# Gate and up products of four feed-forward parts as seven products of quarters instead of eight

## The chip, the cores and the metric

The kernel runs on one core of a Trainium2 chip. The core has five engines that run side by side, each with its own queue of instructions: TensorE (PE in the profile; its weight loads are PEld), VectorE (DVE), ScalarE (ACT), GpSimd (POOL) and SyncE (SP), which here only issues DMA transfers. Instructions of one engine start in order; between engines they wait for semaphores. Data lie in SBUF (128 partitions) or, as results of TensorE, in PSUM (8 banks). The metric is the time of one execution on the device in microseconds; the comparison uses the median of several executions.

## What is computed

A stack of two transformer-like layers over 512 tokens plus 16 meta tokens in front (528), then a second kind of block over the 512 tokens, all in float32 with a model width of 1024. What matters here are its five feed-forward parts, each with a hidden width of 2816:

```python
def swiglu(x, w_gu, w_down):
    gate, up = jnp.split(x @ w_gu, 2, axis=-1)
    return (jax.nn.silu(gate) * up) @ w_down

h = h + 0.5 * swiglu(rms_norm(h, ffn1_norm[l]), ffn1_w_gu[l], ffn1_w_down[l])   # before each mixer
h = h + 0.5 * swiglu(rms_norm(h, ffn2_norm[l]), ffn2_w_gu[l], ffn2_w_down[l])   # behind each mixer
...
x = x + (jax.nn.silu(h2 @ w_ffn_gate[l]) * (h2 @ w_ffn_up[l])) @ w_ffn_down[l]  # in the second block
```

## The kernel before

Activations lie feature-major: a tile holds 128 features on the partitions and all tokens as columns. The feed-forward parts are called a0 and b0 (layer 0), a1 and b1 (layer 1) and c (second block). a0, b0 and a1 run over 528 tokens, in two pieces of 264 columns; b1 and c over 512 in one piece. Their order in time is a0, b0, a1, b1, c, with a mixer ahead of b0, one ahead of b1 and the second block's attention and state-space branches ahead of c.

*Precision.* TensorE is fed in a format that holds fewer bits than float32. So every operand is split in a high part (`whi`, `xh`, `gh`: a copy into the short format) and a remainder (`wlo`, `xl`, `gl`: original minus high part), and each product of a k tile of 128 takes three matmuls (`mm3`, lines 356 to 358): high x high, high weight x low input, low weight x high input.

*The feed-forward part* (`ffn`). A hidden tile j (0 to 21, 128 hidden features) takes the gate product and the up product, 8 k tiles each, in banks of their own. The input is not normed yet; VectorE multiplies both results by the norm's factor R per token as it takes them out of PSUM (`scaled`, line 444), ScalarE makes Silu, VectorE multiplies (line 455), ScalarE and VectorE split the result into gh and gl. After tiles 0 to 8, 9 to 15 and 16 to 21 stand the down products of 8, 7 and 7 hidden tiles, which add to the residual h. R comes from a sum over the squares, which a matmul with ones does after the products of tile 0 (line 396).

*The weights* (`run`). They come in chunks of 128 x 1024 (8 k tiles by 128 columns, 512 KB) into three raw buffers in turn. ScalarE makes the high half (line 218), GpSimd or, for each third chunk, VectorE the remainder (line 319), into four pairs of buffers in turn. `ahead` issues these splits up to four chunks ahead of use, and behind each split the load that takes the raw buffer just read. SP issues loads in order; each waits until its buffer's last reader is done.

What sets the order: the program is a list of items (a hidden tile, a group of down products), each with its chunks; the framework then places the instructions of each engine in an order of its own, worked out beforehand, so code that is written later can stand earlier in an engine's queue.

## Time and profile before

| | us |
|---|---|
| median of 3 runs | 3302.76 |
| lowest, highest | 3295.20, 3303.64 |
| span of the profiled execution | 3300.4 |
| TensorE busy in it | 3250.9 (99%) |
| VectorE, ScalarE, GpSimd busy | 1645.8, 1166.3, 1145.8 |

The profile records one execution; the page has no other time for it than the span from its first to its last instruction. A row of a group gives the line of the kernel, the engine, the operation, out<-in with names, the shape, the count, then busy time in us and the mean of one in ns, and the idle time of the engine just before, with what ended it. Matmuls overlap each other, so their own durations are longer than the time from one start to the next. In the timeline the first number is the start in us, the second the duration.

### The profile page before, as it was taken

The page shows a single profiled execution, that of the slowest core. Times are in us where ns is not written, and L with a number is a line of the kernel's source. Part 1 is how long each engine was busy: PE and PEld are TensorE (multiplying, and loading weights), DVE is VectorE, ACT ScalarE, POOL GpSimd, SP SyncE. Part 2 cuts the span into 40 slices and gives each one's busy share as a digit, 9 for nine tenths or more (in the row PEclk, how much of TensorE's full clock was granted, in tenths as well). Part 3 has the DMA queues.
Part 4 walks back from the last instruction along what each step waited for, and adds up shares of the span by engine and source line. Part 5 has one row for each costly group of instructions (what it writes and reads, how often), then busy time and mean ns, then how long its engine had stood idle before and what let it go on. Part 6 is the DMA issues. An engine that isn't in the chain of part 4 may idle for free. (4 is left out here: it accounts for less than half of the span.)

```text
span 3300.4 us, 49937 instructions
## 1 busy us (share of the span) xinstructions
PE 3250.9 (99%) x20794; PEld 2878.9 (87%) x20794; DVE 1645.8 (50%) x2687; ACT 1166.3 (35%) x1777; POOL 1145.8 (35%) x614
## 2 busy tenths in 40 slices
PE   9999999999999999999999999999999889999999
...
PEclk9999999999999999999998999999999989999999
...
GB/s 183 122 107 110 93 88 39 46 52 65 90 90 96 84 95 87 95 90 90 85 88 58 46 48 63 96 95 96 91 94 148 109 87 58 71 91 95 93 95 80
DMA packets 106514, 289.43 MB, mean 88 GB/s; under 512 B 23088, under 2 KB 32304, under 8 KB 106288
## 3 DMA queue, kind: packets, MB, share of 16 engines
...
## 5 line engine op out<-in xcount | busy, mean ns | idle before, releaser
L319 POOL TENSOR_TENSOR wlo<-raw,whi 128x1024 fp32r<-128x1024 f32 (+1 forms) x346 | 840.6, 2430 | 1797.1 <-ACT whi L218 1758.0
L218 ACT ACTIVATE whi<-raw 128x1024 fp32r<-128x1024 f32 (+1 forms) x504 | 522.6, 1040 | 1536.3 <-PE bank L357 807.0
L356 PE MATMUL bank<-xh,whi 128*128 128x264 f32 (+1 forms) x2816 | 881.1, 313 | 3.7 <-DVE t L444 3.1
L357 PE MATMUL bank<-xl,whi 128*128 128x264 f32 (+1 forms) x2816 | 880.8, 313 | 2.7 <-DVE xl L377 2.6
L358 PE MATMUL bank<-xh,wlo 128*128 128x264 f32 (+1 forms) x2816 | 881.4, 313 | 1.3 <-POOL wlo L319 1.3
L356 PEld LDWEIGHTS bank<-xh,whi 128*128 128x128 f32 x2816 | 530.9, 189 | 37.7 <-DVE t L444 3.5
L357 PEld LDWEIGHTS bank<-xl,whi 128*128 128x128 f32 x2816 | 531.2, 189 | 36.4 <-DVE xl L377 3.5
L358 PEld LDWEIGHTS bank<-xh,wlo 128*128 128x128 f32 x2816 | 530.6, 189 | 33.2 <-POOL wlo L319 1.5
L444 DVE TENSOR_TENSOR t<-bank,R 128x264 f32<-128x264 f32 (+1 forms) x352 | 163.5, 494 | 576.2 <-PE bank L358 571.5
L358 PE MATMUL bank<-gh,wlo 128*128 128x264 f32 (+1 forms) x1408 | 439.6, 312 | 0.0
L356 PE MATMUL bank<-gh,whi 128*128 128x264 f32 (+1 forms) x1408 | 439.3, 312 | 0.0
L357 PE MATMUL bank<-gl,whi 128*128 128x264 f32 (+1 forms) x1408 | 439.1, 312 | 0.0
L541 PE MATMUL bank<-xh,whi 128*128 128x264 f32 (+2 forms) x1224 | 428.0, 350 | 0.0
L541 PE MATMUL bank<-xl,whi 128*128 128x264 f32 (+2 forms) x1224 | 423.6, 346 | 3.0 <-DVE xl L377 3.0
L541 PE MATMUL bank<-xh,wlo 128*128 128x264 f32 (+2 forms) x1224 | 419.5, 343 | 0.0
L356 PEld LDWEIGHTS bank<-gh,whi 128*128 128x128 f32 x1408 | 264.8, 188 | 16.3 <-issue 0.4
L357 PEld LDWEIGHTS bank<-gl,whi 128*128 128x128 f32 x1408 | 264.8, 188 | 16.1
L358 PEld LDWEIGHTS bank<-gh,wlo 128*128 128x128 f32 x1408 | 264.8, 188 | 15.7
L541 PEld LDWEIGHTS bank<-xl,whi 128*128 128x128 f32 (+1 forms) x1224 | 233.9, 191 | 28.9 <-issue 6.5
L541 PEld LDWEIGHTS bank<-xh,whi 128*128 128x128 f32 (+1 forms) x1224 | 233.8, 191 | 25.1 <-issue 5.8
L541 PEld LDWEIGHTS bank<-xh,wlo 128*128 128x128 f32 (+1 forms) x1224 | 233.5, 191 | 24.9 <-issue 8.1
L501 DVE SCALAR_TENSOR_TENSOR h<-bank,h 128x264 f32<-128x264 f32 (+1 forms) x192 | 89.7, 496 | 331.8 <-PE bank L358 331.1
...
## 6 DMA issues: line engine op xcount, KB each, us to landing
raw<-in_w_dram SPq DMA_DIRECT2D x423, 512.0 KB, 3.5
...
```

The costliest lines, as they stand in the source:

```text
L218: i = self.e.activation(out, in_, func, **kw)
L319: e.tensor_tensor(lo[:, :n], t[:, :n], hi[:, :n].bitcast(F32), op=OP.subtract)
L356: mm(p, hi[:, wk, :m], xh[k][:, c0:c1], start=start, stop=False)
L357: mm(p, hi[:, wk, :m], xl[k][:, c0:c1], start=False, stop=False)
L358: mm(p, lo[:, wk, :m], xh[k][:, c0:c1], start=False, stop=stop)
L444: nc.vector.tensor_tensor(t[:, a:b], p, st["R"][:, a:b], op=OP.mult)
L501: nc.vector.scalar_tensor_tensor(hv, q, alpha, hv, op0=OP.mult, op1=OP.add)
L541: self.nc.tensor.matmul(at["ps"], w[:, k0 + k, :m], xx[k][:, a:b], start=k == t == 0, stop=k == nk - 1 and t == 2)
```

## The change

In a1, b0, b1 and c, hidden tiles 5 to 21 are computed in another way. Gate and up weights of a hidden tile together are one matrix of 1024 x 256, the input one of 1024 x tokens. Each is seen as 2 x 2 quarters: the weights by k tiles 0 to 3 and 4 to 7 and by gate and up, the input by k tiles and by first and second half of the tokens. Of the 2 x 2 quarters of the result (gate and up, for the two halves of the tokens) eight quarter products would be the plain way; here seven are taken, of sums and differences of quarters, and the results are put together from partial sums.

- In the input: `sums`, once per part, in tiles 1 to 4 while these run the plain way. Per pair of k tiles (k, k + 4) it makes the normed input itself (x0, x1, gain and R applied), four combinations (ta, tb), and splits all into high and low parts.
- In the weights: `split_seven`, per hidden tile, in four parts: part 0 is chunk g as it is (VectorE), part 1 the half-chunk sums s1 and s2, part 2 s3 and s4 (sums on VectorE, high halves on ScalarE, remainders on VectorE), part 3 half of chunk u (remainder on GpSimd). One buffer pair holds two quarters. A raw buffer is given back only with parts 2 and 3.
- The products: `unit`, in four items per hidden tile. Bank b1 takes four of the seven products one on top of the other; after the first three ScalarE copies what stands there (tu twice, zu), before TensorE may add the next. b3 takes two, b2 one. VectorE puts c1 (gate) and c2 (minus up) together; R is no longer applied here.

The diff, without the lines that only take comments away:

```diff
     def run(self):
         order = [c for it in self.prog for c in it.chunks]
+        loads = [c for u in order for c in (([u] if isinstance(u, str) else u[1:3]) if isinstance(u, str) or u[0] == 0 else [])]
         self.split_of = {}
         raws = {}
+        S = {}
         n_dma = n_split = used = 0
+        nc = self.nc
         def dma(i):
-            idx, nk, m, _ = CHUNKS[order[i]]
+            idx, nk, m, _ = CHUNKS[loads[i]]
             t = self.wp.tile([128, 1024], F32, tag=f"raw{i % self.RAW}", name=f"raw_{i}")
             self.nc.sync.dma_start(t[:, :nk * m], self.ins["w"][idx, :, :nk * m])
-            raws[i] = t
+            raws[loads[i]] = t
+        def two(hi, lo, a, b, src, e):
+            self.sc.activation(hi[:, a:b], src, AF.Copy)
+            e.tensor_tensor(lo[:, a:b], src, hi[:, a:b].bitcast(F32), op=OP.subtract)
+        def split_seven(hi, lo, part, g, u):
+            q0, q1 = slice(0, 512), slice(512, 1024)
+            add = OP.add
+            if part == 0:
+                two(hi, lo, 0, 1024, raws[g], nc.vector)
+                return 0
+            a1, a2 = raws.get(g), raws[u]
+            if part == 1:
+                s1, s2 = S["s1"], S["s2"] = self.alloc("s1"), self.alloc("s2")
+                nc.vector.tensor_tensor(s1[:, q0], a2[:, q0], a2[:, q1], op=add)
+                nc.vector.tensor_tensor(s2[:, q0], s1[:, q0], a1[:, q0], op=add)
+                two(hi, lo, 512, 1024, s1[:, q0], nc.vector)
+                two(hi, lo, 0, 512, s2[:, q0], nc.vector)
+                self.free(S.pop("s1"))
+                return 0
+            if part == 2:
+                s3, s4 = self.alloc("s3"), self.alloc("s4")
+                nc.vector.tensor_tensor(s3[:, q0], a2[:, q0], a1[:, q0], op=add)
+                nc.vector.tensor_tensor(s4[:, q0], S["s2"][:, q0], a1[:, q1], op=add)
+                two(hi, lo, 0, 512, s3[:, q0], nc.vector)
+                two(hi, lo, 512, 1024, s4[:, q0], nc.vector)
+                self.free(s3, s4, S.pop("s2"))
+                raws.pop(g)
+                return 1
+            two(hi, lo, 0, 512, a2[:, q1], nc.gpsimd)
+            raws.pop(u)
+            return 1
         def split(i):
-            _, nk, m, _ = CHUNKS[order[i]]
-            n = nk * m
-            t = raws.pop(i)
             hi = self.wp.tile([128, 1024], F32R, tag=f"hi{i % self.H}", name=f"whi_{i}")
             lo = self.wp.tile([128, 1024], F32R, tag=f"lo{i % self.H}", name=f"wlo_{i}")
-            self.sc.activation(hi[:, :n], t[:, :n], AF.Copy)
-            e = self.nc.vector if i % 3 == 0 and order[i].split(".")[0] not in BUSY else self.nc.gpsimd
-            e.tensor_tensor(lo[:, :n], t[:, :n], hi[:, :n].bitcast(F32), op=OP.subtract)
+            if isinstance(order[i], str):
+                _, nk, m, _ = CHUNKS[order[i]]
+                n = nk * m
+                e = nc.vector if i % 3 == 0 and order[i].split(".")[0] not in BUSY else nc.gpsimd
+                two(hi, lo, 0, n, raws.pop(order[i])[:, :n], e)
+                freed = 1
+            else:
+                nk, n = 8, 1024
+                part, g, u = order[i]
+                freed = split_seven(hi, lo, part, g, u)
             self.split_of[order[i]] = (hi[:, :n].rearrange("p (k m) -> p k m", k=nk),
                                        lo[:, :n].rearrange("p (k m) -> p k m", k=nk))
+            return freed
         def ahead(top):
             nonlocal n_dma, n_split
             while n_split < min(top, len(order)):
-                split(n_split)
+                freed = split(n_split)
                 n_split += 1
-                if n_dma < len(order):
-                    dma(n_dma)
-                    n_dma += 1
+                for _ in range(freed):
+                    if n_dma < len(loads):
+                        dma(n_dma)
+                        n_dma += 1
...
-    # ---- SwiGLU with its residual ----
-    def ffn(self, tag, n, st, alpha, nxt):
-        """st: the normed input's parts; nxt(m): after the residual's tile m is final."""
+    def ffn(self, tag, n, st, alpha, nxt, gname=None, l=0):
         nc = self.nc
         g = {}
+        PLAIN_J = 5 if gname else NJ
+        half = n // 2
+        Y = {}
+        def sums(k):
+            f = slice(0, n)
+            x0, x1 = self.alloc("x0"), self.alloc("x1")
+            for x, kk in ((x0, k), (x1, k + 4)):
+                nc.vector.scalar_tensor_tensor(x[:, f], self.h[kk][:, f], self.gain(gname, l, kk), st["R"][:, f], op0=OP.mult, op1=OP.mult)
+            a, b = self.alloc("ta"), self.alloc("tb")
+            q0, q1 = slice(0, half), slice(half, n)
+            nc.vector.tensor_tensor(a[:, q0], x0[:, q0], x0[:, q1], op=OP.subtract)
+            nc.vector.tensor_tensor(a[:, q1], x1[:, q1], x0[:, q1], op=OP.subtract)
+            nc.vector.scalar_tensor_tensor(b[:, q0], a[:, q1], -1.0, x0[:, q0], op0=OP.mult, op1=OP.subtract)
+            nc.vector.scalar_tensor_tensor(b[:, q1], b[:, q0], -1.0, x1[:, q0], op0=OP.mult, op1=OP.subtract)
+            if k % 2 == 0:
+                Y["b11", k // 2] = self.alloc("b11h", F32R), self.alloc("b11l", F32R)
+            hl = Y["b11", k // 2]
+            d = slice(half * (k % 2), half * (k % 2) + half)
+            self.sc.activation(hl[0][:, d], x0[:, q0], AF.Copy)
+            nc.vector.tensor_tensor(hl[1][:, d], x0[:, q0], self.fl(hl[0][:, d]), op=OP.subtract)
+            Y["B11", k] = [t[:, d] for t in hl]
+            for t, n0, n1 in ((x1, "B21", "B22"), (a, "T1", "T3"), (b, "T2", "T4")):
+                hl = Y["full", n0, k] = self.split_x(t, n, n0, lo="vector")
+                Y[n0, k] = [t[:, q0] for t in hl]
+                Y[n1, k] = [t[:, q1] for t in hl]
+            self.free(x0, x1, a, b)
+        def seventh(ps, w, k0, b, start):
+            hi, lo = w
+            def mm(a, x, first, last):
+                nc.tensor.matmul(ps, a, x, start=start and first, stop=last, skip_group_check=not start)
+            for k in range(4):
+                xh, xl = Y[b, k]
+                mm(hi[:, k0 + k, :], xh, k == 0, False)
+                mm(hi[:, k0 + k, :], xl, False, False)
+                mm(lo[:, k0 + k, :], xh, False, k == 3)
+        E = {}
+        def unit(j, part):
+            w = self.split_of[part, f"{tag}g{j}", f"{tag}u{j}"]
+            q0, q1, f = slice(0, half), slice(half, n), slice(0, n)
+            copy = self.sc.activation
+            if part == 0:
+                b1, b2 = E["b1"], E["b2"] = [self.bank()[:, :half] for _ in range(2)]
+                c1, c2, tu, zu = (E.setdefault(x, self.alloc(x)) for x in ("c1", "c2", "tu", "zu"))
+                seventh(b1, w, 0, "B11", True)
+                copy(tu[:, q0], b1, AF.Copy)
+                seventh(b2, w, 4, "B21", True)
+                nc.vector.tensor_tensor(c1[:, q0], b2, tu[:, q0], op=OP.add)
+                return
+            b1, c1, c2, tu, zu = (E[x] for x in ("b1", "c1", "c2", "tu", "zu"))
+            if part == 1:
+                b3 = E["b3"] = self.bank()[:, :half]
+                seventh(b1, w, 0, "T2", False)
+                copy(tu[:, q1], b1, AF.Copy)
+                seventh(b3, w, 4, "T1", True)
+                copy(zu[:, q0], b3, AF.Copy)
+            elif part == 2:
+                b3 = E["b3"]
+                seventh(b1, w, 0, "T3", False)
+                copy(zu[:, q1], b1, AF.Copy)
+                nc.gpsimd.tensor_tensor(c2[:, q1], zu[:, q0], zu[:, q1], op=OP.add)
+                seventh(b3, w, 4, "B22", False)
+                nc.vector.tensor_tensor(c1[:, q1], b3, tu[:, q1], op=OP.add)
+                s = E["s"] = self.alloc("s")
+                self.sc.activation(s[:, f], c1[:, f], AF.Silu)
+            else:
+                s = E["s"]
+                seventh(b1, w, 0, "T4", False)
+                nc.vector.scalar_tensor_tensor(c2[:, q1], c2[:, q1], -1.0, s[:, q1], op0=OP.mult, op1=OP.mult)
+                nc.vector.scalar_tensor_tensor(c2[:, q0], b1, -1.0, s[:, q0], op0=OP.mult, op1=OP.mult)
+                g[j] = self.split_x(c2, n, "g", lo="vector")
+                self.free(c1, c2, tu, zu, s)
+                E.clear()
+                if j == NJ - 1:
+                    self.free(*Y["b11", 0], *Y["b11", 1])
+                    for key in list(Y):
+                        if key[0] == "full":
+                            self.free(*Y[key])
+                    Y.clear()
...
             t, s = evac_gate(pg, cols)
             evac_up(j, pu, cols, t, s)
-            if j == NJ - 1:
+            if PLAIN_J < NJ and 0 < j < 5:
+                sums(j - 1)
+            if j == PLAIN_J - 1:
                 self.free(st.pop("R"), *st.pop("xh"), *st.pop("xl"))
         def down(t, m2):
...
         c = 0.22 * 3
         def add_gu(j):
-            self.add(2 * KT * c, lambda: gu(j), [f"{tag}g{j}", f"{tag}u{j}"])
+            if j < PLAIN_J:
+                return self.add(2 * KT * c, lambda: gu(j), [f"{tag}g{j}", f"{tag}u{j}"])
+            for part in range(4):
+                self.add(KT * c * (0.25 if part == 3 else 0.5), lambda part=part: unit(j, part), [(part, f"{tag}g{j}", f"{tag}u{j}")])
...
-            self.ffn(f"a{l}", L, st, 0.5, nxt_m)
+            self.ffn(f"a{l}", L, st, 0.5, nxt_m, "ffn1_norm" if l else None, l)
-            self.ffn(f"b{l}", n2, st_f, 0.5, nxt)
+            self.ffn(f"b{l}", n2, st_f, 0.5, nxt, "ffn2_norm", l)
-        self.ffn("c", SEQ, st_c, 1.0, self.store)
+        self.ffn("c", SEQ, st_c, 1.0, self.store, "norm2_g_2", 0)
```

What this moves in the queues, at three places of b0 (numbers in names tell buffers apart; L319 of before is L317 behind the change, L308 is L311, L444 is L576).

VectorE before, in two successive hidden tiles of b0, where t is the scaled product and R the norm's factor:

```order
L444 TENSOR_TENSOR t_1127_11072<-bank_1123_10972,R_1083_10437 128x264 [waits PE_49]
L444 TENSOR_TENSOR t_1127_11072<-bank_1124_10973,R_1083_10437 128x264 [waits PE_49]
L319 TENSOR_TENSOR wlo_141_11085<-raw_141_10846,whi_141_11084 128x1024 [waits DMAHW1_49,Activation_49]
L444 TENSOR_TENSOR t_1127_11072<-bank_1125_10974,R_1083_10437 128x264 [waits PE_49,Activation_49]
L444 TENSOR_TENSOR t_1127_11072<-bank_1126_10975,R_1083_10437 128x264 [waits DVE_49,PE_49]
L455 TENSOR_TENSOR t_1127_11072<-t_1127_11072,s_1128_11075 128x528 [waits DVE_49]
L459 TENSOR_TENSOR gl_1130_11081<-t_1127_11072,gh_1129_11080 128x528 [waits Activation_49]
L444 TENSOR_TENSOR t_1135_11196<-bank_1131_11096,R_1083_10437 128x264 [waits PE_49]
L444 TENSOR_TENSOR t_1135_11196<-bank_1132_11097,R_1083_10437 128x264 [waits PE_49]
```

Only one row here waits for a load, the remainder of a chunk that VectorE has every third time.

VectorE behind the change, from the first add into c1 of tile 10 of b0 on; raw_157 and raw_158 are chunks g and u of tile 11, raw_159 and raw_160 those of tile 12:

```order
L541 TENSOR_TENSOR c1_1259_12236<-bank_1258_12235,tu_1261_12238 128x264 [waits PE_49,Activation_49]
L317 TENSOR_TENSOR wlo_169_12267<-raw_157_12094,whi_169_12266 128x1024 [waits Activation_49]
L317 TENSOR_TENSOR wlo_170_12298<-s1_1264_12299,whi_170_12297 128x512 [waits PE_49,Activation_49]
L317 TENSOR_TENSOR wlo_170_12298<-s2_1265_12300,whi_170_12297 128x512 [waits Activation_49]
L330 TENSOR_TENSOR s1_1278_12437<-raw_160_12346 128x512 [waits DMAHW4_49]
L556 TENSOR_TENSOR c1_1259_12236<-bank_1263_12270,tu_1261_12238 128x264 [waits PE_49]
L317 TENSOR_TENSOR wlo_171_12337<-s3_1267_12338,whi_171_12336 128x512 [waits Activation_49]
L317 TENSOR_TENSOR wlo_171_12337<-s4_1268_12339,whi_171_12336 128x512 [waits Activation_49]
L562 SCALAR_TENSOR_TENSOR c2_1260_12237<-c2_1260_12237,s_1266_12334 128x264 [waits Activation_49,Pool_49]
L563 SCALAR_TENSOR_TENSOR c2_1260_12237<-bank_1257_12234,s_1266_12334 128x264 [waits PE_49]
L331 TENSOR_TENSOR s2_1279_12438<-s1_1278_12437,raw_159_12232 128x512 [waits DMAHW3_49,DVE_49]
L338 TENSOR_TENSOR s3_1281_12476<-raw_160_12346,raw_159_12232 128x512
```

The remainder wlo_169 reads raw_157; s1_1278, three rows on, reads raw_160, which comes into the same of the three buffers, and the add that closes c1 of this tile stands behind it.

SP behind the change, the loads of these chunks:

```order
L311 DMA raw_157_12094<-in_w_dram 128x1024 [waits DMAHW6_49,Pool_49]
L311 DMA raw_158_12208<-in_w_dram 128x1024 [waits DMAHW7_49,DVE_49]
L311 DMA raw_159_12232<-in_w_dram 128x1024 [waits DMAHW0_49,Pool_49]
L311 DMA raw_160_12346<-in_w_dram 128x1024 [waits DMAHW1_49,DVE_49]
L311 DMA raw_161_12370<-in_w_dram 128x1024 [waits DMAHW2_49,Pool_49]
```

raw_160 waits for VectorE, raw_159 and raw_161 for GpSimd. Loads still stand in the order of use, but two of the three buffers hold the chunks of one tile until its parts 2 and 3 are split.

ScalarE behind the change, in the same tile: tu and zu are the copies out of the banks, whi the high halves, s is Silu:

```order
L218 ACTIVATE tu_1261_12238<-bank_1257_12234 128x264 [waits PE_49]
L218 ACTIVATE whi_169_12266<-raw_157_12094 128x1024 [waits DMAHW1_49,PE_49,Activation_49]
L218 ACTIVATE tu_1261_12238<-bank_1257_12234 128x264 [waits PE_49]
L218 ACTIVATE whi_170_12297<-s1_1264_12299 128x512 [waits PE_49,Activation_49]
L218 ACTIVATE zu_1262_12239<-bank_1263_12270 128x264 [waits PE_49]
L218 ACTIVATE whi_170_12297<-s2_1265_12300 128x512 [waits DVE_49]
L218 ACTIVATE zu_1262_12239<-bank_1257_12234 128x264 [waits PE_49]
L218 ACTIVATE whi_171_12336<-s3_1267_12338 128x512 [waits DVE_49,PE_49,Activation_49]
L218 ACTIVATE whi_171_12336<-s4_1268_12339 128x512 [waits DVE_49]
L218 ACTIVATE s_1266_12334<-c1_1259_12236 128x528 [waits DVE_49]
L218 ACTIVATE whi_172_12366<-raw_158_12208 128x512 [waits DMAHW2_49,PE_49,Pool_49]
L218 ACTIVATE gh_1269_12362<-c2_1260_12237 128x528 [waits DVE_49]
```

Before, this queue had two high halves, Silu and gh for a tile; now each copy out of b1 that TensorE waits for has a high half ahead of it or, at the start of a tile, gh of the tile before.

## Rows read from the trace of the kernel before

**Rows 1.** Page: engines, slices of the span, and the chain that ended last.
```profile
span 3300.4 us, 49937 instructions
...
PE 3250.9 (99%) x20794; PEld 2878.9 (87%) x20794; DVE 1645.8 (50%) x2687; ACT 1166.3 (35%) x1777; POOL 1145.8 (35%) x614
...
PE   9999999999999999999999999999999889999999
...
PEclk9999999999999999999998999999999989999999
...
PE 14%; POOL 0%; DVE 0%; issue 0%
PE bank L358 5%; PE bank L357 5%; PE bank L356 5%; POOL ybl L374 0%; PE bank L396 0%; DVE h L501 0%
```

**Rows 2.** Windows over b0 and c: each engine's busy us and instructions.
```profile
core 0: us, PE busy (x) PEld busy (x) DVE busy (x) ACT busy (x) POOL busy (x), PEclk, DMA share, GB/s
930.00:1300.00 370.00, 370.00 (x3040) 370.00 (x3039) 148.33 (x216) 103.62 (x125) 103.22 (x44) 1.00 0.27 92
2940.00:3290.00 350.00, 350.00 (x1500) 281.59 (x1499) 124.53 (x135) 90.82 (x107) 104.54 (x42) 1.00 0.27 94
```

**Rows 3.** Groups by line and form, VectorE: count, busy us, mean ns, idle before.
```profile
L319 DVE TENSOR_TENSOR wlo<-raw,whi 128x1024 fp32r<-128x1024 f32 x133 | 173.9, 1308 | 62.4 <-ACT whi L218 62.2
L444 DVE TENSOR_TENSOR t<-bank,R 128x264 f32<-128x264 f32 x264 | 102.8, 429 | 317.2 <-PE bank L358 316.0 <-ACT s L218 0.7
...
L459 DVE TENSOR_TENSOR gl<-t,gh 128x512 fp32r<-128x512 f32 x44 | 71.3, 1619 | 23.7 <-ACT gh L218 23.7
...
L455 DVE TENSOR_TENSOR t<-t,s 128x512 f32<-128x512 f32 x44 | 30.4, 692 | 1.4
```

**Rows 4.** Groups by line and form, ScalarE, then GpSimd.
```profile
L218 ACT ACTIVATE whi<-raw 128x1024 fp32r<-128x1024 f32 x423 | 446.3, 1058 | 1246.9 <-PE bank L357 617.4 <-issue 488.7 <-PE bank L541 115.2
...
L218 ACT ACTIVATE gh<-t 128x528 fp32r<-128x528 f32 x66 | 42.6, 645 | 47.6 <-DVE t L455 47.6
L218 ACT ACTIVATE s<-t 128x528 f32<-128x528 f32 x66 | 41.8, 633 | 46.7 <-DVE t L444 46.5
...
L218 ACT ACTIVATE k<-bank 64x264 f32<-64x264 f32 x32 | 12.2, 382 | 3.6 <-PE bank L541 3.2
...
L319 POOL TENSOR_TENSOR wlo<-raw,whi 128x1024 fp32r<-128x1024 f32 x290 | 716.4, 2471 | 1484.0 <-ACT whi L218 1448.2 <-PE bank L541 8.8 <-DMA raw<-in_w_dram 8.0
...
L1004 POOL TENSOR_TENSOR X<-zf 128x512 f32<-128x512 f32 x36 | 43.8, 1221 | 16.1 <-PE bank L610 5.5 <-DVE ro L411 2.9 <-PE bank L941 2.7
```

**Rows 5.** Timeline around 1300 us: start, us, engine, line, operands.
```profile
1297.72 2.38 POOL L319 TENSOR_TENSOR wlo<-raw,whi 128x1024 fp32r<-128x1024 f32 x1 [2.73 <-ACT whi L218]
1298.30 2.37 DVE L377 SCALAR_TENSOR_TENSOR xl<-h,gains,xh 128x528 fp32r<-128x528 f32 x1 [1.22 <-ACT xh L218]
...
1300.13 0.33 SPq L308 DMA_DIRECT2D raw<-in_w_dram  x1
...
1300.60 0.69 DVE L425 TENSOR_TENSOR sq<-sq,sq 128x528 f32<-128x528 f32 x1
...
1302.81 1.23 DVE L319 TENSOR_TENSOR wlo<-raw,whi 128x1024 fp32r<-128x1024 f32 x1 [0.59 <-ACT whi L218]
```

**Rows 6.** Weight loads: issues with sizes and landing, and landings of thirteen.
```profile
raw<-in_w_dram SPq DMA_DIRECT2D x423, 512.0 KB, 3.5
...
DMA to landing us min/median/max: 3.3/3.4/4.4
```

**Rows 7.** Waits of the load queue: total us, times, longest.
```profile
SPq L308 <- POOL wlo L319: 2162.3, 339, 22.2
SPq L308 <- DVE wlo L319: 593.7, 138, 16.3
```

**Rows 8.** Timeline after tile 0 of c: factor R and first scaling.
```profile
2936.44 1.02 PE L396 MATMUL bank<-sq,ones 128*128 128x512 f32 x2
...
2942.92 1.29 DVE L444 TENSOR_TENSOR t<-bank,R 128x512 f32<-128x512 f32 x2
```


## The prediction

> **What bounds the kernel now.** I read the page first: TensorE is busy 99% of a span of 3300.4 us, its granted clock at 0.8 or more in every slice (1.00, the level of 2.4 GHz, in the stretches below), and the slices of the feed-forward parts are solid nines [rows 1]. The chain that ended last names hardly anything but TensorE's products [rows 1]. So in these parts each column streamed through TensorE costs time, and VectorE and GpSimd come in only where they make TensorE wait. Next the windows: in the part b0 (528 tokens, "wide" below, as a1) 3040 products of 264 columns fill 370 us, 0.1217 us each; in c (512 tokens, "narrow", as b1) 1500 products of 512 columns fill 350 us, 0.2333 us each. There VectorE is busy for 40% and 36%, GpSimd for 28% and 30% [rows 2]. Third, the durations of what the change adds [rows 3, 4], how VectorE and GpSimd hinder each other [rows 5], and the weight loads: what they wait for and how long they take to land [rows 6, 7].
>
> The profiled span is 2.4 us under the median of the runs, 3302.76; I work out a difference and take it from the median. A measurement of this kernel can tell about 0.3%, 10 us, from no change.
>
> **TensorE, what goes.** A hidden tile now takes 96 products of 264 columns (wide), 96 x 0.1217 = 11.68 us, or 48 of 512 (narrow), 48 x 0.2333 = 11.20 us. Afterwards it takes seven times 12 products of 264 or 256 columns. Wide: 84 x 0.1217 = 10.22 us, 1.46 us less. For 256 columns the trace has no such stream; the two rates give 0.00045 us a column, so 0.1181 us, 9.92 us a tile, 1.28 us less (if 256 cost as much as 264: 10.22 us, 0.98 us less; I take the line, since 264 columns lie next to it). 34 wide and 34 narrow tiles: 49.6 + 43.5 = 93 us, at least 83.
>
> **VectorE, what comes.** In a tile now, VectorE has four scalings out of PSUM (two in a narrow one), a product, a remainder and about two thirds of a 1024-column weight remainder. Afterwards, per tile: the remainder of chunk g (1.22 us; one that nothing hindered took 1.23, the mean is 1.31) [rows 3, 5], four half-chunk sums and four half-chunk remainders of 512 columns (0.69 us by the row of the same size), two adds into c1, two products into c2 (0.43 us by the 264-column row) and the remainder gl (0.70, a little over the 0.69 of 512 columns) [rows 3]. Instructions in a row start 0.07 us before the one ahead has ended: xl ends at 1298.30 + 2.37 = 1300.67, the next starts at 1300.60 [rows 5]. So 512 columns count 0.62: 1.2 + 8 x 0.62 + 4 x 0.43 + 0.63 = 8.5 us of 10.2. That alone fits.
>
> GpSimd adds 1.2 us for its half-chunk remainder (half of 2.4; 512 columns took 1.22) and about 0.65 for its add of 264 columns [rows 4]. This isn't free beside VectorE: with a GpSimd remainder running from 1297.72 to 1300.10, the VectorE remainder that began at 1298.30 ended 0.57 us after it and took 2.37 us [rows 5]; the 512-column gl has a mean of 1.62 us against 0.69 for a product of the same size [rows 3]. I count a GpSimd instruction as time in which VectorE's instructions on two SBUF operands stand still; those that read one operand from PSUM I leave alone (the scalings at 264 columns have a mean of 0.43 us with GpSimd at work beside them) [rows 3]. The Trainium skill has this as a rule (SBUF — State Buffer, section Who interferes with whom): the two engines share a pair of ports, one instruction holds it to its end, and the other engine's waits in full. By that rule the sum below stands; if the two only shared bandwidth, half of GpSimd's time would fall out of it.
>
> **The loop that sets the pace.** In the order of VectorE behind the change, the sum s1 of up-chunk u of tile j+2 stands in tile j, ahead of (wide) or just behind (narrow, mostly) the add that closes c1. That chunk's raw buffer is the one chunk g of tile j+1 leaves: the load waits for VectorE's 1024-column remainder a few instructions earlier. In the trace of before, a load is issued 0.03 us after the remainder that frees its buffer ended (1300.10, 1300.13) [rows 5], and lands 3.3 to 4.4 us later, 3.45 taken [rows 6]. Now the loads wait 2162 and 594 us for GpSimd's and VectorE's remainders and nobody minds, since each chunk is loaded well ahead [rows 7]; afterwards VectorE itself stands behind the load, in order, and everything queued behind s1 with it: c1, so Silu, so c2, so the copy gh on ScalarE, so the copy tu that is next on ScalarE, for which TensorE waits before it adds the third product into the same bank.
>
> Round the loop, wide: s1 0.62, c1 0.43, two half remainders 1.24, c2 0.43 (2.72); GpSimd's half remainder, which ScalarE releases at this point, 1.2; s2, s3, gl, s4 2.49, c1 of the next tile 0.43, remainder of g 1.22 (4.14); load 0.03 + 3.45. Sum 11.54 us a tile, against 10.22 on TensorE: 1.32 us of stall. Narrow: mostly without the first c1, 11.1 us against 9.92: 1.18 us of stall. The idle 3.5 us of VectorE hold the two half remainders and GpSimd's add of the tile; those wait for nothing later.
>
> The loop is closed in 11 of 17 tiles of a part (runs of 4, 7 and 6 tiles between the down products; the last two of a run have no s1 behind a load), and the first of each run starts with VectorE unhurried, so half a stall, 0.6. Wide: 3 x 0.6 + 8 x 1.32 = 12.4 us a part; narrow 3 x 0.6 + 8 x 1.18 = 11.2. Four parts: 47 us given back. Bounds of the loop: GpSimd's instruction outside it, 10.3 us (no stall worth naming); the load at the longest landing, 4.4, 12.5 us (then 22 us a part).
>
> **ScalarE** has per tile 1024 + 5 x 512 columns of high halves, four copies of 264 out of PSUM (0.38), Silu and gh (0.65): 1.06 + 5 x 0.63 + 4 x 0.4 + 1.3 = 7.1 us of 10.2 [rows 4]. It isn't full. Its copies tu and zu come behind at most one high half, 1.06 us, within the 1.46 us of the product between, so I cost it at nothing outside the loop; without that cover it would be up to 0.4 us a copy.
>
> **The sums of the input**, in tiles 1 to 4 of each part: per pair of k tiles 2 x 0.70 + 5 x 0.4 + 3 x 0.65 = 5.4 us of VectorE, and what stands beside it there. From the first scaling, 6.5 us after the ones product that follows tile 0 [rows 8], VectorE has to work off four of these (21.6), the evacuation of tiles 0 to 3 (4 x (4 x 0.4 + 0.7 + 0.63) = 11.7) and 5.5 of weight work (two remainders of 1.22, five halves of 0.62): 38.8 us, and some 6 us of standing still for GpSimd (three remainders of 2.4 fall there): ready at 51 us. TensorE comes to tile 5 at 4 x 11.68 = 46.7 us and needs the last sums about 4 us later. I take 2 us a part, 8 in all; bounds 0 and 8 a part.
>
> **Sum.** 93 - 47 - 8 = 38 us less: 3302.8 - 38 = 3265 us.
>
> **Rivals.**
> *TensorE stays the bound* (the loop is shorter than I reckon, as VectorE gets the ports first or GpSimd falls into its idle time). For it: VectorE's 8.5 us fit; against it: a load that hangs on VectorE and on which VectorE hangs is 3.5 us of idle time that no order hides. 93 less 8 at most, and a few us of stall: 3215 us.
> *Slower: the loop grows past the old tile.* Place: the same wait at s1. Price: loads land in 4.4 us, since two of them overlap when VectorE and GpSimd free their buffers close together, and GpSimd's add (0.65) falls into the loop too: 11.54 + 0.95 + 0.65 = 13.1 wide, 12.7 narrow. Stalls 3 x 1.5 + 8 x 2.9 = 27.7 a part, 111 in four; 93 - 111 - 8 = -26: 3329 us. It decides from a loop of about 12.3 us on. For it: landings up to 4.4 us are in the trace; against it: the median is 3.4, and with about 1 MB a tile the load is what it was.
> *No change*: a loop between 11.9 and 12.5 us, 3293 to 3313 us.
>
> **How the numbers follow.** Loop as reckoned, 3240 to 3292 us: 0.53. TensorE bound, 3205 to 3239: 0.17. No change: 0.11. Slower: 0.19. So faster 0.70, same 0.11, slower 0.19. The likeliest case's own range is 3240 to 3292; the range given, 3212 to 3313, takes in most of the first rival and all of no change, and leaves out the slower one and the best corner.
>
> **What would show it.** TensorE has 84 products a tile at 0.118 to 0.122 us; in the runs of tiles 5 to 8, 9 to 15 and 16 to 21 one stall of TensorE a tile, at the first product that waits for ScalarE's copy tu, of 1.0 to 1.5 us from the second or third tile of a run on and none in its last; VectorE idle before s1 with a load as the releaser, 3 us in sum a tile; tiles of 11.1 to 11.6 us there, near 10.2 at the ends of runs. If VectorE doesn't wait for loads at s1, the first rival holds. If the tiles are over 12.3 us, or TensorE waits 5 us and more before the first product of tile 5, I was too kind to VectorE. If the granted clock falls in these stretches, none of the prices hold.

## The result and the profile after

The kernel with the change takes 3261.0 us (median of 4 runs, 3257.55 to 3261.63), the one before 3298.98 us beside it (4 runs); the ratio is 0.9885, 95% interval 0.987 to 0.9901. That is 38 us less, and 3265 us was predicted. The profiled span is 3259.7 us against 3300.4 [rows 1]: 40.7 us less.

The page after: engines, granted clock, and the chain that ended last.

```profile
span 3259.7 us, 53075 instructions
...
PE 3174.7 (97%) x21610; PEld 2869.4 (88%) x21610; DVE 2038.7 (63%) x3417; ACT 1407.6 (43%) x2385; POOL 1080.1 (33%) x656
...
PEclk9999999999999999999998999999999999999999
...
PE 9%; DVE 3%; DMA 1%; issue 1%; ACT 0%; POOL 0%; DVEq 0%; ACTq 0%
```

TensorE went from 99% to 97% although it has less to do: it waits now. VectorE went from 1645.8 to 2038.7 us, and VectorE and DMA stand in the chain, where hardly anything but TensorE stood [rows 1]. TensorE's granted clock looks as before in these tenths of 40 slices; that it fell in four places shows only in finer windows (below, tile 5).

*Where the time went.* From the timeline I took, for each of the 68 tiles made of seven products, the time from its first product to that of the next tile (at the end of a run: to its own last product and one interval more). Part b0: 16.46, 10.25, 10.63, 10.39 | 10.24, 10.24, 11.14, 11.38, 11.19, 11.05, 10.30 | 10.23, 10.25, 10.72, 11.11, 11.19, 10.28 us. Part c: 17.52, 9.93, 10.10, 10.12 | 9.94, 9.93, 9.94, 10.98, 11.01, 10.97, 10.01 | 9.93, 10.02, 9.93, 10.82, 10.99, 10.05 us. a1 is like b0 and b1 like c. All 68 take 737.3 us; 34 x 11.68 + 34 x 11.20 = 777.9 were needed before at the two rates of that trace, so 40.6 us less: the whole change of the span lies in these tiles. An unhindered tile takes 10.22 (wide) and 9.92 us (narrow), so 68 of them 684.8. The rest, 52.5 us, is lost in two places: 25.6 us in the four first tiles (tile 5: 16.46, 16.66, 15.27, 17.52 us, of 40.3 unhindered), and 26.9 us in tiles 6 to 21 (671.4 us), in which 26 of the 64 tiles take over 10.5 us.

The durations that were worked out, as groups of the trace after (count, busy us, mean ns, idle before):

```profile
L317 DVE TENSOR_TENSOR wlo<-s,whi 128x512 fp32r<-128x512 f32 x272 | 184.4, 706 | 27.4 <-ACT whi L218 22.8
L331 DVE TENSOR_TENSOR s<-s,raw 128x512 f32<-128x512 f32 x68 | 75.0, 1103 | 0.0
...
L317 POOL TENSOR_TENSOR wlo<-raw,whi 128x512 fp32r<-128x512 f32 x68 | 92.4, 1359 | 386.3 <-ACT whi L218 356.0 <-DVE wlo L317 30.3
L554 POOL TENSOR_TENSOR c<-zu 128x264 f32<-128x264 f32 x34 | 26.0, 765 | 166.0 <-ACT zu L218 166.0
```

Half remainders and half sums take 0.68 to 0.71 us where GpSimd leaves VectorE alone, as the rows of that size had said [rows 3]; s2 (L331), beside which GpSimd's half remainder runs, takes 1.10. GpSimd's own two are longer than the 1.2 and 0.65 us counted [rows 4]: 1.36 for the half remainder, 0.77 for the add of 264 columns, and 1.08 for that of 256.

*Tiles 6 to 21.* Waits of the whole span after: what waited for what, us in sum, times, the longest.

```profile
DVE s L330 <- DMA raw<-in_w_dram: 109.0, 58, 6.1
...
PE bank L521 <- ACT tu L218: 33.6, 29, 4.8
```

L330 is the sum s1. It waits for its load 58 times, and TensorE for ScalarE's copy tu 29 times. One turn of the loop in b0, timeline:

```profile
1101.74 0.69 DVE L330 TENSOR_TENSOR s<-raw 128x512 f32<-128x512 f32 x1 [2.10 <-DMA raw<-in_w_dram]
1102.35 0.42 DVE L556 TENSOR_TENSOR c<-bank,tu 128x264 f32<-128x264 f32 x1
...
1104.05 1.41 POOL L317 TENSOR_TENSOR wlo<-raw,whi 128x512 fp32r<-128x512 f32 x1 [3.80 <-DVE wlo L317]
1104.24 0.42 DVE L563 SCALAR_TENSOR_TENSOR c<-bank,s 128x264 f32<-128x264 f32 x1
1104.59 1.43 DVE L331 TENSOR_TENSOR s<-s,raw 128x512 f32<-128x512 f32 x1
1104.70 0.64 ACT L218 ACTIVATE gh<-c 128x528 fp32r<-128x528 f32 x1 [0.72 <-DVE c L563]
1105.25 0.37 ACT L218 ACTIVATE tu<-bank 128x264 f32<-128x264 f32 x1
1105.68 0.39 PE L521 MATMUL bank<-T2h,whi 128*128 128x264 f32 x1 [0.83 <-ACT tu L218]
1105.94 0.68 DVE L338 TENSOR_TENSOR s<-raw,raw 128x512 f32<-128x512 f32 x1
...
1108.10 1.21 DVE L317 TENSOR_TENSOR wlo<-raw,whi 128x1024 fp32r<-128x1024 f32 x1
1109.34 0.33 SPq L311 DMA_DIRECT2D raw<-in_w_dram  x1
1112.96 0.69 DVE L330 TENSOR_TENSOR s<-raw 128x512 f32<-128x512 f32 x1 [1.94 <-DMA raw<-in_w_dram]
```

s1 starts at 1101.74, having waited 2.10 us for its load; the add that closes c1 (L556) is right behind it. Over c2, gh and tu this reaches TensorE at 1105.68, 0.83 us late. The remainder of chunk g ends at 1109.31, the load is issued at 1109.34 and lands for s1 at 1112.96. The turn is 11.22 us, 7.57 of VectorE and 3.65 of load.

*Tile 5.* Timeline of b0 around its start at 975.5 us:

```profile
974.56 0.70 DVE L418 TENSOR_TENSOR T1l<-ta,T1h 128x528 fp32r<-128x528 f32 x1
...
975.86 0.68 DVE L339 TENSOR_TENSOR s<-s,raw 128x512 f32<-128x512 f32 x1
...
976.60 0.33 SPq L311 DMA_DIRECT2D raw<-in_w_dram  x1
...
979.94 0.69 DVE L330 TENSOR_TENSOR s<-raw 128x512 f32<-128x512 f32 x1 [2.01 <-DMA raw<-in_w_dram]
...
981.15 0.77 DVE L576 TENSOR_TENSOR t<-bank,R 128x264 f32<-128x264 f32 x2
...
983.16 0.64 ACT L218 ACTIVATE gh<-t 128x528 fp32r<-128x528 f32 x1 [5.16 <-DVE t L587]
...
984.66 0.37 ACT L218 ACTIVATE tu<-bank 128x264 f32<-128x264 f32 x1
985.08 0.59 PE L521 MATMUL bank<-T1h,whi 128*128 128x264 f32 x1 [3.54 <-ACT tu L218]
985.47 0.42 PE L521 MATMUL bank<-T1l,whi 128*128 128x264 f32 x1
985.69 0.42 PE L521 MATMUL bank<-T1h,wlo 128*128 128x264 f32 x1
```

The last input sums end at 975.26, when TensorE begins tile 5. Sums of tile 6 (s1, L330, and s3 behind it), the first of which waits 2.01 us for a load, stand in VectorE's queue ahead of tile 4's last scalings (981.15); gh of tile 4 waits for these, tu is queued behind gh, TensorE waits for tu. The load went out at 976.60, right behind the end, at 976.54, of s4 of tile 5 (L339), which in the code is the last to read chunk g and so gives its buffer back: the load was late because VectorE itself was.

The wait of 3.54 us puts the next product 3.7 us late, and b0 loses 6.2 us here. The rest is TensorE's clock: behind the wait the products start 0.22 us apart, in place of 0.1217. In three windows (start and end, length, TensorE's busy time and products, granted clock, two figures of the DMA):

```profile
975.00:983.60 8.60, 6.54 (x54) 1.00 0.36 122
983.80:990.40 6.60, 5.32 (x24) 0.50 0.29 82
990.60:1000.00 9.40, 9.40 (x79) 1.00 0.25 72
```

The clock is at 1.00 (2.4 GHz) while TensorE works and into its wait, then at 0.50 (1.2 GHz), then at 1.00 again; before the change it was 1.00 in all of this stretch. Over the four tiles 5 its mean is 0.79, 0.80, 0.89 and 0.81; from product to product, 16.2 of the 25.6 us there are waits and 9.3 slower products. In tiles 6 to 21, where no wait is longer than 1.24 us, it stays at 1.00.

### The profile page after: what moved, and what is told of

The parts are those of the page before. It is cut to its first block, busy times and chain, and to the rows that moved or that the text cites. A ratio compares the mean times of both kernels' runs of the same rounds, so it can differ in the third digit from the quotient of the medians.

```text
span 3259.7 us, 53075 instructions
## 1 busy us (share of the span) xinstructions
PE 3174.7 (97%) x21610; PEld 2869.4 (88%) x21610; DVE 2038.7 (63%) x3417; ACT 1407.6 (43%) x2385; POOL 1080.1 (33%) x656
## 5 line engine op out<-in xcount | busy, mean ns | idle before, releaser
L317 POOL TENSOR_TENSOR wlo<-raw,whi 128x1024 fp32r<-128x1024 f32 (+3 forms) x320 | 713.7, 2232 | 1488.9 <-ACT whi L218 1427.6
L218 ACT ACTIVATE whi<-raw 128x1024 fp32r<-128x1024 f32 (+2 forms) x504 | 491.5, 979 | 873.7 <-PE bank L401 329.1
L400 PE MATMUL bank<-xh,whi 128*128 128x264 f32 (+1 forms) x1184 | 356.5, 302 | 5.5 <-DVE t L576 4.6
L401 PE MATMUL bank<-xl,whi 128*128 128x264 f32 (+1 forms) x1184 | 355.2, 301 | 2.7 <-DVE xl L421 2.5
L402 PE MATMUL bank<-xh,wlo 128*128 128x264 f32 (+1 forms) x1184 | 355.1, 301 | 1.3 <-POOL wlo L317 1.3
L317 DVE TENSOR_TENSOR wlo<-raw,whi 128x1024 fp32r<-128x1024 f32 (+1 forms) x184 | 231.4, 1257 | 80.6 <-ACT whi L218 80.3
L400 PEld LDWEIGHTS bank<-xh,whi 128*128 128x128 f32 x1184 | 223.1, 189 | 14.3 <-DVE t L576 5.0
L218 ACT ACTIVATE whi<-s 128x512 fp32r<-128x512 f32 x272 | 162.8, 626 | 168.1 <-PE bank L521 98.5
L401 PEld LDWEIGHTS bank<-xl,whi 128*128 128x128 f32 x1184 | 223.6, 189 | 11.3 <-DVE xl L421 3.5
```

The source lines that it names most:

```text
L218: i = self.e.activation(out, in_, func, **kw)
L317: e.tensor_tensor(lo[:, a:b], src, hi[:, a:b].bitcast(F32), op=OP.subtract)
L400: mm(p, hi[:, wk, :m], xh[k][:, c0:c1], start=start, stop=False)
L401: mm(p, hi[:, wk, :m], xl[k][:, c0:c1], start=False, stop=False)
L402: mm(p, lo[:, wk, :m], xh[k][:, c0:c1], start=False, stop=stop)
```

## The experiments

Twelve kernels, compared by their profiled span, by the four tiles 5 (65.9 us after the change, 40.3 unhindered) and by tiles 6 to 21 (671.4 us, 644.5 unhindered), and by their ratio to the kernel before. The span also holds what the clock does outside these tiles, some us from one execution to the next; the tiles are the cleaner measure.

**e1: up-chunks in buffers of their own.**

```
...
-            t = self.wp.tile([128, 1024], F32, tag=f"raw{i % self.RAW}", name=f"raw_{i}")
+            if loads[i] in own:
+                t = raws[loads[i]] = self.alloc("ua"), self.alloc("ub")
+                for q in range(2):
+                    nc.sync.dma_start(t[q][:, :512], self.ins["w"][idx, :, 512 * q:512 * q + 512])
+                return
...
```

> Edit: the up chunk u of every seven-product tile no longer goes through the ring of three raw buffers. It gets two buffers of its own, filled by two 256 KB loads, so its load no longer waits for VectorE to release a raw buffer; all else is as in the changed kernel (3261.0 us, profiled span 3259.7). Theory A (the stalls of tiles 6 to 21 are a loop: VectorE releases a raw buffer, the load of u lands 3.5 us later, VectorE waits for it with its other work queued behind): the 26.6 us of stall in tiles 6 to 21 go, and some 5 us of the stall in tile 5; a span of 3225 to 3235 us, wide tiles at 10.2 to 10.4 us in the middle of the runs, where 11.0 to 11.4 stand now. Rival B (VectorE and ScalarE work as such, or their order, sets 11.0 to 11.4 us, loads or not): no change, 3255 to 3265. Rival C (the loads, now free to start early, collide with the loads of the gate chunks): slower, 3265 to 3285.

Median 3236.34 us, ratio 0.9799 (0.9777 to 0.9821), span 3230.4. Tiles 6 to 21 take 653.1 us, and from tile 9 on 527.0 in place of 548.6; 4.0 us of the 8.6 that are left lie in one tile 6. VectorE's order is another one here too (e4 comes back to this), but 25 times in tiles 6 to 21 s1 still stands ahead of the add that closes c1; it waits there 5.8 us in all, and no tile from 9 on takes over 10.4 us. So the load of u is a link of the loop; B and C fall. The tiles 5 kept 60.7 us, which theory A had about right in size (5.2 less), but all of it came in the narrow parts, and the tile 6 that loses 4.0 us stands behind the tile 5 that gained most, in b1.

**e2: the input sums one tile earlier.**

```
-            if PLAIN_J < NJ and 0 < j < 5:
-                sums(j - 1)
+            if PLAIN_J < NJ and j < 4:
+                sums(j)
```

> Edit: the input sums of the four quarters are computed behind tiles 0 to 3 and not behind tiles 1 to 4; the same instructions, one tile earlier, so that VectorE has tile 4 to work off what is left. Theory A (the 25.6 us that TensorE loses in tile 5 of the four parts come from VectorE being behind with the input sums when the products of quarters begin): the four tiles 5 fall from 16.5, 16.7, 15.3 and 17.5 us to about 11 to 12, so 15 to 22 us less, a span of 3238 to 3245. Rival B (the loss belongs to the first seven-product tile itself, its first remainders and first load, wherever the sums stand): no change, 3256 to 3264. Rival C (the backlog moves with the sums and TensorE loses the time in tiles 1 to 4): tile 5 falls and the span stays at 3255 to 3265.

Median 3255.72, ratio 0.9864 (0.9847 to 0.9882), span 3246.6 (of the fastest of four runs). Tiles 5: 17.25, 17.23, 14.13, 12.85 us; 4.4 us less in sum, all in the narrow parts, which fits no expectation. The timeline of b0 says why:

```profile
978.14 0.69 DVE L338 TENSOR_TENSOR s<-raw,raw 128x512 f32<-128x512 f32 x1 [2.28 <-DMA raw<-in_w_dram]
978.75 0.76 DVE L576 TENSOR_TENSOR t<-bank,R 128x264 f32<-128x264 f32 x2
...
980.90 0.37 ACT L218 ACTIVATE tu<-bank 128x264 f32<-128x264 f32 x1
981.32 0.59 PE L521 MATMUL bank<-T2h,whi 128*128 128x264 f32 x1 [5.03 <-ACT tu L218]
```

Now it is s3 (L338) of tile 6 that waits for its load, still ahead of tile 4's scalings; TensorE waits 5.03 us. So the place of a sum in the queue matters in tile 5 too.

**e3: tile 5 left plain.**

```
-        PLAIN_J = 5 if gname else NJ
+        PLAIN_J = 6 if gname else NJ
```

> Edit: tile 5 of each part keeps its eight plain products per row block; the seven products begin with tile 6. The input sums stay behind tiles 1 to 4. Each part gives up one seven-product tile: 1.46 us of TensorE in each of the two wide parts, 1.28 in each of the two narrow ones, 5.5 us in all. Theory A (VectorE's backlog of input sums is what stalls the first seven-product tile): with one tile between, the first seven-product tile loses 0 to 2 us a part and not 5.4 to 7.6: 25.6 - 4 + -5.5, so 14 to 20 us less, a span of 3240 to 3246. Rival B (the first seven-product tile loses its time wherever it stands): 5.5 us more, 3263 to 3267.

Median 3228.53, ratio 0.979 (0.9774 to 0.9805), span 3233.8. The first seven-product tiles take 10.24, 10.23, 9.93 and 9.92 us: nothing is lost there. B falls. The span is 6 us better than A's, the median 11; tiles 6 to 21 are unchanged (673.4). What is left, some 8 us of the profiled span outside all these tiles, goes with the clock: TensorE stood at its lower level there for 47 us, in the run after the change for 63, and 16 us less at half the rate are some 8 us by estimate. Whether the change of tile 5 has to do with that is not shown.

**e4: the half remainder on VectorE.**

```
-            two(hi, lo, 0, 512, a2[:, q1], nc.gpsimd)
+            two(hi, lo, 0, 512, a2[:, q1], nc.vector)
```

> Edit: the half remainder of the fourth product piece (part 3 of each seven-product tile), 512 columns, runs on VectorE in place of GpSimd; nothing else moves. Theory A (GpSimd's half remainder costs VectorE about 0.75 us beside it, as s2 at 1.43 us against s3 at 0.68, and in tile 5 it is itself held up to 6.95 us by VectorE's run of work, so that the load behind it is late): the loop's period stays within 0.2 us (VectorE gains 0.75 and pays about 0.65), s2 falls to about 0.7 us, tile 5 loses 2 to 3 us less in each part; span 3245 to 3256. Rival B (VectorE is the full engine of the loop and any work added to it costs its length): 0.65 us more in each tile of the run that the loop closes, some 28 to 44 of them, 3275 to 3290.

Median 3232.39, ratio 0.9797 (0.9784 to 0.981), span 3232.7. Tiles 6 to 21 take 646.4 us, with none over 10.50: the loop's stall is gone, which neither theory expected. s2 did fall (mean 0.77 us against 1.10), but even the whole 0.75 us that s2 lost in the turn shown cannot bring 11.22 to 10.24. The edit had moved something else as well. The same place in b0:

```profile
1110.26 0.43 DVE L556 TENSOR_TENSOR c<-bank,tu 128x264 f32<-128x264 f32 x1 [0.86 <-PE bank L521]
...
1112.40 0.43 DVE L563 SCALAR_TENSOR_TENSOR c<-bank,s 128x264 f32<-128x264 f32 x1
1112.74 0.68 DVE L317 TENSOR_TENSOR wlo<-raw,whi 128x512 fp32r<-128x512 f32 x1
1113.34 0.68 DVE L330 TENSOR_TENSOR s<-raw 128x512 f32<-128x512 f32 x1
```

The framework works out VectorE's order anew for each kernel. Here s1 (L330) stands behind the add that closes c1 and both products into c2, with no wait, where after the change it stood ahead of all three. In 28 of tiles 6 to 21 s1 stands like this; where it does not, it waits 9.6 us in all, against 64.1 in these tiles after the change. So two explanations were open: the place of s1, or GpSimd out of VectorE's way. e5 and e7 take one each.

**e5: s1 held to its place, GpSimd left as it was.**

```
-                nc.vector.tensor_tensor(s1[:, q0], a2[:, q0], a2[:, q1], op=add)
+                self.tc.keep_in_program_order(nc.vector.tensor_tensor(s1[:, q0], a2[:, q0], a2[:, q1], op=add))
```

> Edit: the sum s1 of each seven-product tile is held to its place in the written order of VectorE's queue (issue order alone, no wait): it stands behind the 1024-column remainder of its own tile and no longer ahead of the add that closes c1 of the tile two before it. The order of TensorE, GpSimd and SyncE is as in the changed kernel, GpSimd's half remainder stays where it was. Theory A (the stalls of tiles 6 to 21 come from s1 standing too early in VectorE's queue: it waits 2 us for its load with c1, c2 and the copies queued behind it): the 26.6 us go, s3, which then is the first reader of the load, stands 2.5 us later and waits for it 0 to 0.5 us; tile 5 stays at 15 to 17 us, since there s3 of tile 6 waits for the load ahead of tile 4's last scalings; span 3232 to 3240. Rival B (GpSimd's half remainder and the 0.75 us that it costs VectorE beside it set the pace, which is why the kernel with that remainder on VectorE took 3232.4 us): 0 to 5 us less, 3254 to 3260.

Median 3239.46, ratio 0.981 (0.979 to 0.983), span 3238.0. Tiles 6 to 21: 648.0 us. Theory A's number, with GpSimd's remainder where it was; B falls. In b0, as expected, s3 is now the first reader of the load, and stands behind both products into c2:

```profile
1100.13 0.43 DVE L556 TENSOR_TENSOR c<-bank,tu 128x264 f32<-128x264 f32 x1 [0.32 <-PE bank L521]
...
1102.29 0.42 DVE L563 SCALAR_TENSOR_TENSOR c<-bank,s 128x264 f32<-128x264 f32 x1
1103.66 0.69 DVE L338 TENSOR_TENSOR s<-raw,raw 128x512 f32<-128x512 f32 x1 [0.95 <-DMA raw<-in_w_dram]
```

It even waits 0.95 us in this turn, more than the 0 to 0.5 expected, and TensorE loses nothing. Tile 5 stays at 65.3 us.

**e6: s1 and s3 held.** The same call around the sum s3 as well.

```
-                nc.vector.tensor_tensor(s3[:, q0], a2[:, q0], a1[:, q0], op=add)
+                self.tc.keep_in_program_order(nc.vector.tensor_tensor(s3[:, q0], a2[:, q0], a1[:, q0], op=add))
```

> Edit: as the one before, and s3, the other reader of up-chunk u, is held to its place in the written order too. Now tile 4's last scalings stand in VectorE's queue ahead of the first sums of tile 6. Theory A (place in the queue, in tile 5 as well: sums of tile 6 and their wait for a load stand ahead of tile 4's evacuation, on which the copy tu and TensorE's third product of tile 5 hang): the stalls of tiles 6 to 21 gone as before, and 2 to 5 us less in each tile 5; span 3212 to 3230. Rival B (tile 5's loss is VectorE's backlog of input sums alone): tile 5 stays within 1 us of 16.5, 16.7, 15.3 and 17.5, span 3231 to 3238. Rival C (later sums make the weight halves late for TensorE): weight waits appear in TensorE's waits, span above 3240.

Median 3223.79, ratio 0.9772 (0.9758 to 0.9785), span 3222.0. Tiles 6 to 21: 645.8 us; tiles 5: 12.46, 12.33, 15.29, 14.94, 10.9 us less than after the change, 4.0, 4.3 and 2.6 in three parts and nothing in b1. Theory A holds but for b1, B and C fall as the whole story. In the two wide tiles 5 TensorE waits 1.96 and 1.84 us in place of 3.54, and the clock stays at 1.00: over the four tiles 5, waits fall from 16.2 to 11.5 us and slower products from 9.3 to 3.2, so that more than half of the 10.9 us is clock. The groups of s1 and s3:

```profile
L330 DVE TENSOR_TENSOR s<-raw 128x512 f32<-128x512 f32 x68 | 46.5, 684 | 0.0
L338 DVE TENSOR_TENSOR s<-raw,raw 128x512 f32<-128x512 f32 x68 | 46.2, 680 | 0.0
```

In all 68 tiles neither waits for a load at all; after the change s1 waited 109.0 us.

**e7: remainder on VectorE, GpSimd kept as busy.**

```
             two(hi, lo, 0, 512, a2[:, q1], nc.vector)
+            d = self.alloc("dum")
+            nc.gpsimd.tensor_tensor(d[:, q0], hi[:, q0].bitcast(F32), hi[:, q0].bitcast(F32), op=OP.subtract)
...
```

> Edit: half remainder of part 3 on VectorE (as in the kernel that took 3232.4 us), and GpSimd makes a subtraction of the same 512 columns beside it, released by the same ScalarE copy, into a buffer that nothing reads. So GpSimd is as busy beside VectorE as in the changed kernel, while VectorE's order stays that of the 3232.4 us kernel but for a few rows, in which s1 stands behind the add of c1 or behind both c2. Theory A (what helped was the new place of s1 in VectorE's queue): GpSimd's instruction stretches one of VectorE's by some 0.7 us a tile, which fits into its idle time; span 3230 to 3240. Rival B (what helped was that GpSimd no longer takes the ports there): the stalls of tiles 6 to 21 come back, all or most of 26.6 us; span 3250 to 3262.

Median 3234.56, ratio 0.9804 (0.979 to 0.9817), span 3233.1; tiles 6 to 21: 647.6 us. GpSimd's extra instruction does stretch VectorE's:

```profile
1111.91 1.04 POOL L347 TENSOR_TENSOR dum<-whi 128x512 f32<-128x512 f32 x1 [2.35 <-ACT whi L218]
1112.18 1.31 DVE L317 TENSOR_TENSOR wlo<-raw,whi 128x512 fp32r<-128x512 f32 x1
```

The half remainder takes 1.20 us in the mean against 0.68 in e4, and of tiles 6 to 21 none is longer than in e4 by more than 0.12 us. B falls: in e4 it was the new order that helped in these tiles, as e5 has it from the other side. The tiles 5 of b1 and c are 1.7 and 1.8 us longer than in e4 (16.91 and 16.66 us); 2.5 of these 3.4 us are slower products behind the wait, and what made the waits longer I have not followed.

**e8: half of the input sums.**

```
...
-            if PLAIN_J < NJ and 0 < j < 5:
+            if PLAIN_J < NJ and j in (1, 2):
                 sums(j - 1)
+            if PLAIN_J < NJ and j == 2:
+                for key in list(Y):
+                    if key[0] not in ("b11", "full"):
+                        Y[key[0], key[1] + 2] = Y[key]
...
```

> Edit: the input sums are computed for two of the four pairs of k tiles only, behind tiles 1 and 2, and the products read those two twice (two pairs of the input are left out of the result). TensorE's work and the order of the seven products are unchanged; VectorE has some 11 us less to do ahead of tile 5 and nothing of it behind tiles 3 and 4. Theory A (VectorE's backlog of input sums is what makes tile 5 late): the four tiles 5 fall from 16.5, 16.7, 15.3, 17.5 to 10.2 to 11.5 us; some 20 us less, span 3236 to 3242. Theory B (sums of tile 6 stand ahead of tile 4's evacuation in VectorE's queue and wait for a load there, backlog or not, as the kernel with the sums one tile earlier suggests, whose wide tiles 5 stayed at 17.2): tiles 5 fall by at most 1 to 3 us each, span 3248 to 3258.

Median 3233.76, ratio 0.9801 (0.9787 to 0.9814), span 3228.3. Tiles 5: 10.22, 10.24, 9.98, 9.89 us, 40.3 in sum: nothing is lost, as A expected, and the clock is 1.00 in all four. Tiles 6 to 21 stay at 672.1. With VectorE not behind, sums ahead of tile 4's scalings cost nothing, even with a wait of 3.50 us for a load among them (b0, TensorE begins tile 5 at 978.6):

```profile
970.34 0.69 DVE L330 TENSOR_TENSOR s<-raw 128x512 f32<-128x512 f32 x1 [3.50 <-DMA raw<-in_w_dram]
...
978.51 0.77 DVE L576 TENSOR_TENSOR t<-bank,R 128x264 f32<-128x264 f32 x2 [0.67 <-PE bank L402]
```

So the two losses are independent: this edit takes the one in tile 5 and leaves the other whole; e5 does the reverse.

**e9: s1 and s3 held, tile 5 plain** (the edits of e6 and e3).

> Edit: s1 and s3 held to their places, and the seven products begin with tile 6 (tile 5 plain, 5.5 us more of TensorE in all). Theory (two causes that add up: in tiles 6 to 21 the place of s1 and s3 in VectorE's queue, in the first seven-product tile VectorE's backlog of input sums, of which 14.9 us are left in the kernel with s1 and s3 held): both gone, 3223 - 14.9 + 5.5: 3210 to 3218, first seven-product tiles at 9.9 to 10.5 us. Rival (what is left in tile 5 is not backlog, and moves to tile 6): 3226 to 3230.

Median 3223.46, ratio 0.9785 (0.977 to 0.9799), span 3216.8: the profiled run is within the range of the theory, the median is no better than e6's. The first seven-product tiles (6) take 10.64, 11.03, 10.82, 10.83 and tiles 6 to 8 131.6 us, where e3 has 124.2: right behind the input sums the written order is worse than the framework's.

**e10: s1 and s3 held, sums early** (the edits of e6 and e2).

> Edit: s1 and s3 held to their places, and the input sums stand behind tiles 0 to 3 and not 1 to 4. Theory A (with the sums of tile 6 behind tile 4's evacuation, VectorE has a tile more to work the backlog off): tiles 5 fall from 12.5, 12.3, 15.3, 14.9 to 10.2 to 11.5 us, span 3207 to 3214, the lowest of all, as no TensorE work is added. Rival B (as without the holding, the wide tiles keep their loss, since TensorE waits there for tile 4's own evacuation in any case): 3215 to 3222.

Median 3225.85, ratio 0.9791 (0.9777 to 0.9804), span 3223.9. Tiles 5: 12.98, 13.86, 16.25, 14.44 us. A falls: the same sums one tile earlier don't help. Why less work for VectorE there does (e8) and earlier work does not, I have not settled.

**e11: the load of u twice as long.**

```
...
-            self.nc.sync.dma_start(t[:, :nk * m], self.ins["w"][idx, :, :nk * m])
+            for _ in range(2 if loads[i] in own else 1):
+                self.nc.sync.dma_start(t[:, :nk * m], self.ins["w"][idx, :, :nk * m])
```

> Edit: in the changed kernel, each load of an up-chunk u of a seven-product tile is issued twice, the second into the same buffer behind the first, so that it lands about 3.5 us later than now (7 us in place of 3.5). Nothing else moves. Theory A (the load of u is a link of the loop: its length adds to the loop's period in full): the loop goes from 11.2 to about 14.7 us wide and from 11.0 to 14.5 narrow; it closes in some 10 to 12 tiles a part with 4.5 us of stall each, and the tiles 5 lose some 3 us more: 180 to 220 us in place of 26.6, span 3415 to 3460. Rival B (the load is hidden or only happens to end last; VectorE's and GpSimd's work sets the period): 0 to 20 us more, 3260 to 3280.

Median 3269.64, ratio 0.9922 (0.9909 to 0.9936), span 3269.9; tiles 6 to 21: 678.4 us, 7 more. A's number is far off, and "nothing else moves" was wrong. In b0:

```profile
1098.33 0.69 DVE L333 TENSOR_TENSOR s<-raw 128x512 f32<-128x512 f32 x1 [1.03 <-DMA raw<-in_w_dram]
...
1101.62 0.68 DVE L342 TENSOR_TENSOR s<-s,raw 128x512 f32<-128x512 f32 x1
...
1109.79 0.69 DVE L333 TENSOR_TENSOR s<-raw 128x512 f32<-128x512 f32 x1 [2.07 <-DMA raw<-in_w_dram]
```

The framework drew VectorE's instructions on the chunk together: from s1 to the last that reads g, now s4 (L342), 3.97 us, then 7.49 from there to the next s1, a turn of 11.46. The load's part went up by 3.8 us and VectorE's down by 3.6, from 7.57. As a test of how the loop's terms add up it is inconclusive; it shows again that an edit elsewhere moves VectorE's order.

**e12: both repairs, the first run left alone.** Tile 5 plain, and s1 and s3 held from tile 9 on.

```
+            hold = self.tc.keep_in_program_order if int(u.split("u")[-1]) >= 9 else lambda ins: ins
...
+                hold(nc.vector.tensor_tensor(s1[:, q0], a2[:, q0], a2[:, q1], op=add))
...
```

> Edit: the seven products begin with tile 6, and s1 and s3 are held to their places from tile 9 on only (the second and third run of tiles between the down products); tiles 6 to 8 keep the order that the framework gives. In the kernel with both and all tiles held, tiles 6 to 8 took 131.5 us in the four parts, in the one with plain tile 5 and nothing held 124.1, while tiles 9 to 21 took 526.7 against 549.4. Theory (the two repairs add, if the first run after the sums is left alone): 7.4 us less than that kernel's profiled span of 3216.8: a span of 3207 to 3212, median of the runs 3208 to 3218, the lowest of all. Rival (holding later tiles changes the first run again, or something else takes its place): 3217 to 3226.

Median 3216.55 (3210.12 to 3220.15), ratio 0.9757 (0.9744 to 0.977), the lowest of all: 44 us below the changed kernel, by medians of different sittings. Tiles 6 to 8 take 124.4, tiles 9 to 21 526.6 us, as expected; the span, 3214.2, is 2 us over, so that lies outside these tiles.

## Why the prediction was right, and where only the sum was

*TensorE, 93 us: right but for the clock.* Unhindered tiles take 10.21 to 10.25 us and 9.86 to 9.93, where 10.22 and 9.92 were worked out; the rate for 256 columns, 0.1181 us, taken from the line through the two known rates, holds. In the four tiles 5 one of the signs of being wrong came: the granted clock fell to 0.50 behind TensorE's wait, products of 0.1217 us took 0.22, and that cost 9.3 us, for which the sum has no term.

*The loop, 47 us: right in mechanism, mis-sized; it cost 26.9.* s1 waits for the load of u, the load for VectorE's remainder, and TensorE for tu, as described. Of the turn 11.54 us were reckoned (wide) and 11.22 measured, 11.1 and 11.0 narrow. GpSimd's half remainder was the term that was too long: it was counted at 1.2 us and cost 0.75, s2 at 1.43 us against s3 at 0.68. It ran from 1104.05 to 1105.46, and 0.54 us of that lay beside the two products into c2, of which the first had begun at 1103.90 and the second (L563) reads PSUM; at 0.42 us each neither was held. The rule of the Trainium skill cited there (SBUF — State Buffer, section Who interferes with whom) agrees, as s2 ended only after GpSimd; what was wrong was to take all of GpSimd's time as standing still. The larger part of the error is the count: 44 tiles were to be stalled, 12 of them at half, and 26 were. VectorE seems to begin a run ahead, and by a turn of 11.22 us against 10.22 it loses 1 us a tile against TensorE; in the longer runs the first two tiles (wide) or three (narrow) lose nothing; I had given this one tile at half.

*The input sums, 8 us: the term that was too small; tile 5 lost 25.6.* VectorE was reckoned to be ready at 51 us, about when TensorE needs the last sums. In b0 the sums are in fact ready at 975.26, when TensorE begins tile 5: that part of the reckoning was not too kind. What it left out is what else is queued there: tile 4's scalings stood behind sums of tile 6 and a wait for a load, which went out late because VectorE was late with s4 of tile 5, and gh and tu stood behind the scalings. The waits that came of this are 16.2 of the 25.6 us, the clock that fell behind them 9.3. e6 takes 10.9 of the 25.6 by the order alone; e8 takes all of it by giving VectorE less to do there, e3 by giving it a tile more of time. The four parts lost 6.2, 6.4, 5.4 and 7.6 us, all within the bound of 8 a part; the value taken, 2, was the wrong one.

*The sum.* 55 us of stall were forecast and 52.5 came: two errors, +20 and -18, cancel. The total was right by more luck than its terms were.

*The rivals.* TensorE as the bound (3215 us) did not happen, but e12 gets there: the reason given against it, that no order hides a load on which VectorE hangs, is wrong. A sum that stands some instructions later hides it (e5, e6). The slower rival did not occur: in the turn of b0 shown the load took 3.65 us, and GpSimd's add (1110.86 to 1111.63) fell into VectorE's wait.
